# Where the two operands of every matmul lie within 128 bytes: a transformer block pair with 9,040 wide matmuls

## The chip, the cores and the metric

The kernel runs on one core of one Trainium2 chip. The metric is the device time of one execution in microseconds (us); the figure of a kernel is the median of several runs. One further execution of the kernel was profiled, and all rows below come from it. It is the same instruction stream, but its time is its own.

## The reference, cut to what matters

The reference chains two transformer blocks on 256 tokens of width 2,048, all in fp32. The first block has a projection of width 11,776, sliding-window attention, retention, a merge, and a layer ("peer") that picks 128 experts for each token out of 16,384 single-row experts. The second has a projection, an attention with forget gates, a recurrent branch, a mixture of 32 experts of width 256 in 4 groups, and a gated output.

```python
proj = xn @ w_in[layer]                                  # 256 x 2048 by 2048 x 11776
y_a = sliding_window_attention(...) @ w_attn_branch[layer]
y_r = retention(...) @ w_ret_branch[layer]
h = h + merged @ w_out[layer]
qry = (xt @ w_query).reshape(T, H, 2, PEER_HALF_DIM)     # peer: scores, top 16 of 128 twice, top 16 of 256
act = jax.nn.gelu(jnp.einsum('td,thkd->thk', xb, expert_down[ib]))
y = jnp.einsum('thk,thkd->td', gb * act, expert_up[ib])
...
for e in range(N_EXPERTS):                               # second block, 32 experts
    hid = jax.nn.silu(t @ w_gate[e]) * (t @ w_up[e])
    out = out + (hid @ w_down[e]) * comb[:, e:e + 1]
```

Nearly all of the arithmetic is these matrix products, with weights that are read from memory once.

## The kernel before, in words

**How a product is made.** Every wide product is done in three matmuls on operands that are split in two fp32r parts: a high part (`hi`) and the rest (`lo`). Activations lie in the pool `big` as split, transposed tiles (`xhi` and `xlo`, `rhi`, `mhi`, `hhi`, `zhi`, `nhi`, `yhi`, the sorted expert inputs `xs`). Weights come by DMA as fp32 tiles (`raw`, `rawg`, `rawd`) from the queue of SyncE (SP), are cast to `whi` by ScalarE (line 253) and the difference `wlo` is made by VectorE (line 254). Then TensorE runs, for each of 16 slices `k` of 128 rows and each half `t` of the tokens, lines 282 to 284:

```python
TE.matmul(ps[:, t, :], h_, hi, start=st, stop=False)
TE.matmul(ps[:, t, :], h_, lo, start=False, stop=False)
env["mm"] = TE.matmul(ps[:, t, :], l_, hi, start=False, stop=en)
```

The first operand after the output is the stationary one, 128 by 128, loaded into the array by a weight load of its own; the second is the moving one, 512 columns as a rule. So a stationary operand is a slice of an activation tile and the moving one is a slice of a weight tile. In `mm_tr` (lines 293 to 295) it is the other way round: a slice of the weights is stationary and 256 columns of activations move. The up-projection of the peer layer (`ua`, `ub`, lines 807 to 809) has dense coefficients `chi` and `clo` as stationary operands; the expert layers have `xs` (lines 1281 to 1283, output `pgu`) and the hidden layer `hhl` (lines 1306 to 1308, output `oa`). One product of the second block (`pv`, output of a 1,032-wide projection) has weight tiles of 344 columns. Attention and transposes use plain fp32 matmuls, in which one instruction of the code becomes two records.

**Stages.** In order: input projection, attention, retention, merge and output of block one (up to about 780 us of the span); the query projection `pq`; routing and the gather of single expert rows (`row`, 8 KB a token, by GpSimd's indirect DMA), with the dot products on VectorE; 32 rounds of the up-projection with gathers of 2 KB pieces (`urow`) beside it; block two's projections and attention; the 32 experts; the gated output. The program's order on each engine is fixed when it is built.

**Where tiles lie.** Pools are laid one after the other in each partition: `cst`, `big`, `sm`, `wr` (raw weights), `ws` (split weights), then what belongs to a stage: `wka`, `wkp`, `wkx`, `wkm`, `wkl` for work tiles and `wr`/`ws` of that stage. A tile of a pool starts where the one before it ends, in units of 32 bytes. Two unused pieces, `pad`, stand in `cst` (32 bytes) and `sm` (two of 32 bytes). In the built program of the kernel before, `big` starts at byte 23,040 and `wr` at byte 141,056, and every stationary and every moving operand of the fp32r matmuls starts at a multiple of 128 bytes. The one exception is `pv`: a weight tile there holds two slices of 344 columns, 1,376 bytes each, so that the second slice starts 96 bytes above a multiple of 128.

Of the kernel before, what the change touches and what calls it, by code (L numbers as in the profile page):

```python
# [9 lines left out]
F32 = mybir.dt.float32  # L10
F32R = mybir.dt.float32r
# [8 lines left out]
P = 128  # L20
# [55 lines left out]
def build(ctx: ExitStack, tc: tile.TileContext, A, out, taps=None, stop=None):  # L76
# [5 lines left out]
    cst = ctx.enter_context(tc.tile_pool(name="cst", bufs=1))  # L82
    big = ctx.enter_context(tc.tile_pool(name="big", bufs=7))
    sm = ctx.enter_context(tc.tile_pool(name="sm", bufs=2))
# [3 lines left out]
    env = {}  # L88
# [36 lines left out]


    cc = cst.tile([P, NKEEP], F32, name="cc")
    cst.tile([P, 8], F32, name="pad")
    sm.tile([P, 8], F32, tag="pad", name="pad")
    nc.sync.dma_start(cc[:, 0:128], A["c_const"][:, 0:128])  # L130
    vecs = w4([P, P], name="vecs")
    nc.scalar.dma_start(vecs[0:16, :], A["attn_norm"].rearrange("(r c) -> r c", c=P))
# [425 lines left out]
    coef = pk[:, 768:1024].rearrange("p (t k) -> p t k", t=2)  # L558
    eidx = env["wk"].tile([P, 2, 8, 16], I32, tag="eidx", name="eidx", bufs=1)
    iota16 = iota[:, 0:16]  # L560

    def route(t, hd):
        sc = sc_t[t][:, hd]
# [434 lines left out]
    for b in range(2):  # L998
# [20 lines left out]
        for hd in range(4 * b, 4 * b + 4):  # L1019
# [21 lines left out]
            PT = env["wk"].tile([P, 384], F32, tag="PT", name="PT2")  # L1041
# [145 lines left out]
    new_phase("m", raws=3, splits=1)  # L1187
    Pmm = env["wk"].tile([P, 2, 2, 512], F32R, tag="Pmm", name="Pmm", bufs=1)
    Pm = Pmm[:, 0]
    t4 = sm.tile([P, 2, 4], F32, tag="t4", name="t4")  # L1190
    V.tensor_tensor(out=t4, in0=prk[:, 0:8].rearrange("p (t g) -> p t g", t=2), in1=oh, op=ALU.mult)
    V.tensor_reduce(out=rk[:, :, 0:1], in_=t4, axis=AX.X, op=ALU.add)
# [278 lines left out]
```

## Time and profile before

| | |
|---|---|
| runs | 3,212.75, 3,214.78 and 3,214.96 us; median 3,214.78 us |
| the profiled execution | 3,219.45 us, of which the span of the program is 3,217.7 us |
| matmul records in it | 12,368 (and as many weight loads) |

How to read the rows further down: a page of the profile gives for each engine its busy time (PE is TensorE's matmuls, PEld its weight loads, DVE VectorE, ACT ScalarE, POOL GpSimd, SP SyncE), and the span in 40 equal slices with a digit for the busy tenths. PEclk is the granted clock of TensorE in tenths of its full 2.4 GHz. Windows give for one stretch its length, then busy time and number of instructions (x) of PE, PEld, DVE, ACT and POOL, then the granted clock, the mean busy share of the DMA engines and what they moved in GB/s. Waits name who waited for whom, the sum in us, how often, and the longest. Timeline rows begin with the start and the length in us. Matmuls are pipelined and their shown ends are modelled; what a matmul costs in a dense stream is the distance from its start to the next one's. Groups of instructions end with their number, the busy time and the mean in ns.

### The profile page before, as it was taken

Reading aid. Unit: us, or ns where it says so; the run is one execution under the profiler, and the core shown is the slowest. Engines: PE = TensorE matmul, PEld = TensorE weight load, DVE = VectorE, ACT = ScalarE, POOL = GpSimd, SP = SyncE. Lnnn points to the kernel's source line nnn. Section 1 sums busy time; section 2 is a strip of 40 time slices with the busy share of each in tenths; the row PEclk is TensorE's granted clock in tenths of the full one; section 3 lists DMA queues with packets and bytes.
Section 4 is the critical chain, followed back from the end, with each engine's and each line's share of the span. In section 5 each row is a group of like instructions: output and inputs, shape, how many; then the busy total and the mean of one; then the engine's idle time right before and its main releaser. Section 6 shows DMA issues by size and latency. Waiting matters only on the chain. (4 is left out here: it accounts for less than half of the span.)

```text
span 3217.7 us, 35193 instructions
## 1 busy us (share of the span) xinstructions
PE 2555.4 (79%) x12368; PEld 2141.8 (67%) x12368; DVE 2535.2 (79%) x3682; ACT 1542.9 (48%) x2212; POOL 879.8 (27%) x575
## 2 busy tenths in 40 slices
PE   8999999999910004400399999999999999999999
PEld 7788888888810003300388888889987787878777
DVE  6656544555999999999988888887575799999974
ACT  5534444444310105441244444457445677778764
POOL 0000000000376686667766666620000000000000
PEclk9999999999965555555699999999999999999999
DMA  6455555565899999999789999974654599999964
GB/s 239 151 182 162 184 191 195 187 220 197 328 352 363 331 427 387 376 342 419 285 306 334 335 334 334 334 263 142 204 190 139 201 338 348 381 344 379 348 226 167
DMA packets 302522, 898.22 MB, mean 279 GB/s; under 512 B 20736, under 2 KB 42240, under 8 KB 268288
## 3 DMA queue, kind: packets, MB, share of 16 engines
q1 hardware_dynamic: 226560, 542.88, 48.1%
q0 software_dynamic: 57760, 335.65, 27.3%
q10 hardware_dynamic: 18016, 17.35, 1.6%
q8 instruction: 99, 1.62, 0.2%
q14 instruction: 87, 0.71, 0.1%
HBM read 887.42 MB, written 8.39 MB: 278 GB/s over the span
## 5 line engine op out<-in xcount | busy, mean ns | idle before, releaser
L254 DVE TENSOR_TENSOR wlo<-raw,whi 128x1024 fp32r<-128x1024 f32 (+1 forms) x538 | 648.5, 1208 | 453.1 <-ACT whi L253 446.9
L253 ACT CAST whi<-raw 128x1024 fp32r<-128x1024 f32 (+1 forms) x538 | 559.5, 1041 | 686.9 <-PE pj L284 255.6
L621 DVE CUSTOM_DVE_ANT_0 row<-row,hn 128x2048 f32<-128x2048 f32 x256 | 579.7, 2291 | 6.1 <-DMA row<-in_peer_expert_down_dram,eidx 5.7
L612 POOL DMA_INDIRECT row<-in_peer_expert_down_dram,eidx x256 | 508.4, 1986 | 265.8 <-DVE dots L621 100.7
L199 POOL TENSOR_TENSOR r<-rstdv,mhalf 128x2 f32<-128x2 f32 x5 | 4.5, 890 | 1508.9 <-DVE rstdv L225 1508.9
L612 POOL DMA_INDIRECT urow<-in_peer_expert_up_dram,eidx x256 | 322.8, 1261 | 197.7 <-DVE h L771 143.8
L254 DVE TENSOR_TENSOR wlo<-rawg,whi 128x1024 fp32r<-128x1024 f32 x256 | 313.1, 1225 | 35.1 <-ACT whi L253 10.3
L253 ACT CAST whi<-rawg 128x1024 fp32r<-128x1024 f32 x256 | 270.0, 1056 | 97.9 <-PE pgu L1283 68.6
L282 PE MATMUL pj<-whi,xhi 128*128 128x512 f32 x736 | 289.4, 393 | 1.3 <-ACT whi L253 1.3
L283 PE MATMUL pj<-wlo,xhi 128*128 128x512 f32 x736 | 288.6, 392 | 0.0
L284 PE MATMUL pj<-whi,xlo 128*128 128x512 f32 x736 | 288.2, 392 | 0.0
L639 PE MATMUL pcf<-cc,pk 128*128 128x128 f32 x2 | 0.9, 460 | 340.7 <-DVE pk L626 340.7
L639 PEld LDWEIGHTS pcf<-cc,pk 128*128 128x128 f32 x2 | 0.4, 182 | 341.5 <-issue 177.8
L1282 PE MATMUL pgu<-wlo,xs 128*128 128x512 f32 x512 | 199.8, 390 | 3.1 <-DVE wlo L254 3.1
L1281 PE MATMUL pgu<-whi,xs 128*128 128x512 f32 x512 | 200.0, 391 | 0.0
L1283 PE MATMUL pgu<-whi,xs 128*128 128x512 f32 x512 | 199.2, 389 | 0.0
L771 DVE SCALAR_TENSOR_TENSOR h<-urow,pk,h 128x512 f32<-128x512 f32 x256 | 191.8, 749 | 4.5
L254 DVE TENSOR_TENSOR wlo<-rawd,whi 128x1024 fp32r<-128x1024 f32 x128 | 154.1, 1224 | 12.1 <-ACT whi L253 1.1
L282 PEld LDWEIGHTS pj<-whi,xhi 128*128 128x128 f32 x736 | 138.5, 188 | 29.5 <-ACT whi L253 1.7
L284 PEld LDWEIGHTS pj<-whi,xlo 128*128 128x128 f32 x736 | 138.4, 188 | 28.1
L283 PEld LDWEIGHTS pj<-wlo,xhi 128*128 128x128 f32 x736 | 138.4, 188 | 27.7
L253 ACT CAST whl<-raw 128x1024 fp32r<-128x1024 f32 x96 | 101.2, 1056 | 113.5 <-PE ua L809 83.0
(547 smaller groups left out, 6302.0 us busy)
## 6 DMA issues: line engine op xcount, KB each, us to landing
raw<-in_w_in_dram SPq DMA_DIRECT2D x124, 1024.0 KB
raw<-in_peer_expert_up_dram SPq DMA_DIRECT2D x96, 1024.0 KB
rawg<-in_w_expert_gate_dram SPq DMA_DIRECT2D x128, 512.0 KB
rawg<-in_w_expert_up_dram SPq DMA_DIRECT2D x128, 512.0 KB
rawd<-in_w_expert_down_dram SPq DMA_DIRECT2D x64, 1024.0 KB
raw<-in_w_out_dram SPq DMA_DIRECT2D x32, 1024.0 KB
raw<-in_w_ret_branch_dram SPq DMA_DIRECT2D x16, 1024.0 KB
raw<-in_w_peer_query_dram SPq DMA_DIRECT2D x16, 1024.0 KB
```

The costliest lines, as they stand in the source:

```text
L199: G.tensor_tensor(out=dst, in0=v, in1=mhalf[:, 0:n], op=ALU.pow)
L253: S.copy(hi, raw)
L254: env["last"] = V.tensor_tensor(out=lo, in0=raw, in1=hi.bitcast(F32), op=ALU.subtract)
L282: TE.matmul(ps[:, t, :], h_, hi, start=st, stop=False)
L283: TE.matmul(ps[:, t, :], h_, lo, start=False, stop=False)
L284: env["mm"] = TE.matmul(ps[:, t, :], l_, hi, start=False, stop=en)
L612: G.indirect_dma_start(out=dst, out_offset=None, in_=src, in_offset=bass.IndirectOffsetOnAxis(ap=idx, axis=0))
L621: V.tensor_tensor_reduce(out=row[:, i, :], in0=row[:, i, :], in1=hn[:, t, :], scale=1.0, scalar=0.0, op0=ALU.mult, op1=ALU.add, accum_out= ...
L771: V.scalar_tensor_tensor(out=h[:, t, 1536:2048], in0=row[:, k, :], scalar=coef[:, t, c0 + k:c0 + k + 1], in1=h[:, t, 1536:2048], op0=ALU.m ...
L1281: TE.matmul(o_, xh, hi[:, :, i, :], start=k == 0, stop=False)
L1282: TE.matmul(o_, xh, lo[:, :, i, :], start=False, stop=False)
L1283: TE.matmul(o_, xl, hi[:, :, i, :], start=False, stop=k == NK - 1)
```

## The change

The unused pieces change, and no others. In `cst` the piece grows from 32 to 96 bytes, and those of `sm` go, so that `big` starts 64 bytes later (byte 23,104) while `sm` and all behind it stay where they were. In `wkp` an unused piece of 64 bytes stands behind `eidx`, ahead of the tiles `chi` and `clo`. In `wkm` one of 64 bytes stands ahead of `esg` and `hhl`, and a second behind them, ahead of the raw and split weights of that stage; the two lines for `esg` and `hhl` in between only fix the order in which the pool lays them out.

```diff
     cc = cst.tile([P, NKEEP], F32, name="cc")
-    cst.tile([P, 8], F32, name="pad")
-    sm.tile([P, 8], F32, tag="pad", name="pad")
+
+    cst.tile([P, 24], F32, name="pad")
     nc.sync.dma_start(cc[:, 0:128], A["c_const"][:, 0:128])
...
     iota16 = iota[:, 0:16]
+    env["wk"].tile([P, 16], F32, tag="pad", name="pad", bufs=1)
...
     Pm = Pmm[:, 0]
+    for i in range(2):
+        env["wk"].tile([P, 16], F32, tag="pad%d" % i, name="pad", bufs=1)
+        if i == 0:
+            env["wk"].tile([P, 256], F32, tag="esg", name="esg")
+            env["wk"].tile([P, 2, 2, P], F32R, tag="PT", name="hhl")
```

On all five engines the instructions, their order and their waits are the same in both built programs. What differs is where operands start, counted from the last multiple of 128 bytes:

| matmuls | stationary before, after | moving before, after |
|---|---|---|
| lines 282 to 284 on `big` tiles, 512 columns | 0, 64 | 0, 0 |
| the same, `pv`, 344 columns | 0, 64 | 0 or 96, 0 or 96 |
| lines 807 to 809 (`chi`, `clo`) | 0, 64 | 0, 0 |
| lines 1281 to 1283 (`xs`), 1306 to 1308 (`hhl`) | 0, 64 | 0, 0 |
| lines 293 to 295 (`mm_tr`), 256 columns | 0, 0 | 0, 64 |
| `pxs` (256 columns), `plT` (256) | 0, 64 | 0, 0 |
| `pun` (512 columns, 64 of them) | 0, 0 | 0, 64 |
| `pu` (512 columns, 48 of them) | 0, 0 | 0, 0 |

DMAs into `big` (the gathered rows `row` and `urow` above all) start 64 bytes above a multiple of 256 after the change, and at a multiple of 256 before. The raw weights of the expert stage start 128 bytes above a multiple of 256 in three of their six buffers, and at a multiple before; the other raw tiles stay.

## Rows read from the trace of the kernel before

**Rows 1.** The page: engines' busy time, and 40 slices of the span.
```profile
PE 2555.4 (79%) x12368; PEld 2141.8 (67%) x12368; DVE 2535.2 (79%) x3682; ACT 1542.9 (48%) x2212; POOL 879.8 (27%) x575
...
PE   8999999999910004400399999999999999999999
...
PEclk9999999999965555555699999999999999999999
```

**Rows 2.** Windows by stage: PE, PEld, DVE, ACT, POOL; clock, DMA, GB/s.
```profile
80.00:780.00 700.00, 699.87 (x3159) 575.32 (x3158) 383.36 (x463) 310.34 (x373) 5.53 (x8) 1.00 0.56 184
...
880.00:1300.00 420.00, 56.64 (x281) 48.45 (x280) 415.55 (x770) 74.83 (x174) 297.96 (x148) 0.54 0.96 374
...
1590.00:2110.00 520.00, 515.99 (x2335) 428.93 (x2335) 451.66 (x682) 252.02 (x399) 330.48 (x265) 0.99 0.93 322
2110.00:2560.00 450.00, 433.96 (x2490) 380.23 (x2490) 312.21 (x565) 259.35 (x382) 12.23 (x11) 0.99 0.53 180
2560.00:3060.00 500.00, 494.92 (x2214) 404.78 (x2213) 461.02 (x444) 386.76 (x420) 0.00 (x0) 1.00 0.96 357
3060.00:3217.00 157.00, 143.06 (x621) 115.97 (x619) 100.49 (x108) 84.81 (x109) 0.69 (x1) 0.95 0.54 193
```

**Rows 3.** Waits in three stretches: first block, up-projection, experts (two rows).
```profile
ACT whi L253 <- PE pj L284: 229.5, 134, 4.6
...
ACT whi L253 <- PE ua L809: 67.8, 49, 1.7
...
ACT whi L253 <- PE pgu L1283: 79.5, 199, 4.6
...
SPq L1271 <- DVE wlo L254: 241.3, 113, 9.2
```

**Rows 4.** One window inside the input projection, 512-column matmuls alone.
```profile
545.00:613.00 68.00, 68.00 (x301) 56.31 (x300) 31.77 (x27) 28.72 (x29) 0.00 (x0) 1.00 0.58 192
```

**Rows 5.** Timeline of the up-projection: start us, length us, engine, line.
```profile
1800.18 0.39 PE L807 MATMUL ua<-whi,chi 128*128 128x512 f32 x1
1800.19 0.19 PEld L808 LDWEIGHTS ua<-wlo,chi 128*128 128x128 f32 x1
...
1800.41 0.39 PE L808 MATMUL ua<-wlo,chi 128*128 128x512 f32 x1
```

**Rows 6.** Timeline of TensorE, 256-column matmuls, eleven in a row.
```profile
2224.74 0.28 PE L294 MATMUL prg<-zlo,whi 128*128 128x256 f32 x1
...
2225.94 0.28 PE L295 MATMUL prg<-zhi,wlo 128*128 128x256 f32 x1
```

**Rows 7.** Timeline of TensorE, 512 columns just behind a break, seven matmuls.
```profile
740.61 0.39 PE L283 MATMUL pwo<-wlo,mhi 128*128 128x512 f32 x1
...
742.00 0.39 PE L283 MATMUL pwo<-wlo,mhi 128*128 128x512 f32 x1
```

**Rows 8.** Timeline of TensorE, plain fp32: two passes of 512, two of 256.
```profile
94.35 1.02 PE L426 MATMUL po<-PT,qkv_a 128*128 128x512 f32 x2
95.21 0.59 PE L410 MATMUL psc<-qkv_a 128*128 128x256 f32 x2
...
2353.96 0.59 PE L1045 MATMUL po<-PT,wv 128*128 128x256 f32 x2
2354.39 0.38 PE L1046 MATMUL po<-PT,wv 128*128 128x128 f32 x2
```

**Rows 9.** Timeline of TensorE in `pv`, 344 columns, every sixth matmul.
```profile
2262.21 0.32 PE L282 MATMUL pv<-whi,zhi 128*128 128x344 f32 x1
...
2263.15 0.32 PE L282 MATMUL pv<-whi,zhi 128*128 128x344 f32 x1
...
2264.10 0.32 PE L282 MATMUL pv<-whi,zhi 128*128 128x344 f32 x1
```

**Rows 10.** Groups of TensorE's instructions by line: number, busy us, mean ns.
```profile
L282 PE MATMUL pj<-whi,xhi 128*128 128x512 f32 x736 | 289.4, 393 | 1.3 <-ACT whi L253 1.3
...
L1281 PE MATMUL pgu<-whi,xs 128*128 128x512 f32 x512 | 200.0, 391 | 0.0
...
L295 PE MATMUL pq<-hhi,wlo 128*128 128x256 f32 x256 | 75.5, 295 | 8.6 <-DVE wlo L254 8.6
...
L293 PE MATMUL prx<-zhi,whi 128*128 128x256 f32 x128 | 37.3, 291 | 0.0
...
L282 PE MATMUL pb<-whi,aT 128*128 128x512 f32 x64 | 24.9, 389 | 0.0
```

## The prediction

> **What bounds the kernel now.** I read the page first, then windows by stage, then who waits for whom, then the timeline of TensorE alone. On the page TensorE is busy in nine tenths or more of nearly every slice up to 780 us and again from about 1,600 us; between them VectorE is, and TensorE's granted clock falls to about half, the 1.2 GHz level [rows 1]. The windows turn that into stages: TensorE covers 699.9 of 700 us in the first block, 516 of 520 in the up-projection, 434 of 450 in block two's projections, 495 of 500 in the experts and 143 of 157 at the end, all at a granted clock of 0.95 to 1.00, the 2.4 GHz level; VectorE covers 415.6 of the 420 us of the gather stage [rows 2]. The waits say the same from the other side: in the first block, the up-projection and the experts ScalarE's casts wait for TensorE to give a split buffer back, and SP waits for VectorE to free a raw buffer before it loads the next weights [rows 3]. So in about 2,300 of 3,217.7 us a faster TensorE is a faster kernel, until the next engine is reached. That is VectorE in the experts, at 461 of 500 us, and DMA there, 0.96 busy; in the first block VectorE is at 383 of 700 [rows 2].
>
> What a matmul costs there is its distance to the next. In a window of the input projection 300 weight loads, one a matmul, fit in 68.00 us: 226.7 ns each [rows 4]. The 256-column ones are 1.20 us apart over ten, 120 ns each [rows 6]. The difference, 106.7 ns for 256 columns, is 0.417 ns a column, which is the 2.4 GHz level. Both widths then have the same rest: 226.7 less 512 columns at 0.417 (213.3) is 13.3 ns, and 120 less 106.7 is 13.3 ns. This rest is the only thing that the change can touch.
>
> **What the rest may be.** Each matmul carries a weight load that starts with it and takes 0.19 us, inside the 0.23 us of its stream [rows 5]. Both read operands that lie in the same partitions. Three rows speak for a collision between them rather than a fixed cost. Just behind a break the same shape takes 1.39 us for six, 232 ns each, 5 ns more than in the steady stream [rows 7]; a fixed cost would not vary. Plain fp32 matmuls, which feed their columns at half the rate (0.86 us for two passes of 512, so 0.84 ns a column), have no such rest: passes of 256 take 0.43 us for two, half of that to the 10 ns that the rows show, with a weight load beside each as well [rows 8]. And the rest does not grow with the width, as a cost per weight load would not. One row speaks against a large effect of the address: in `pv` the moving slices of every second `k` start 96 bytes above a multiple of 128, and six matmuls take 0.94 us there and 0.95 us where they start at the multiple [rows 9], a rest of 13.3 and 15.0 ns over 344 columns (143.3 ns).
>
> The Trainium skill, in TensorE: Matmul & The Clock Gate, Step-by-step: what each phase is for, says that TensorE reads its moving and its stationary operand through two independent ports, so that loading the next weights takes nothing from the running matmul. By that rule no address matters and the sum is zero. The same page, Back-to-back issue gap, gives N/2.4 + 2.5 ns for a warm matmul alone, 216 ns for 512 columns; the trace has 226.7, so by this figure about 11 ns of the rest would be open to the change.
>
> **The change part by part.** No instruction, order or wait changes. With each edit the stationary operand goes to 64 bytes past a multiple of 128 while the moving one stays, or the reverse in `mm_tr`; the edits have one price, ns a matmul, and differ in counts.
>
> Price: no row shows operands 64 bytes apart. The bounds are nothing, which is the nearest row in address (`pv`, 96 bytes apart, hardly moved), and the whole rest of 13.3 ns, which plain fp32 shows to be possible. I take half, 6.7 ns. The rows are about equally far from both ends: a shift of 96 bytes removes 1.7 of 15 ns, and half-rate streams lose nothing.
>
> Counts: the 512-column lines come in threes, 13 groups of them, from `pj` with 736 to `pb` on `aT` with 64 [rows 10]; with all of them, the last `pgt`, `pun` and `pu` it is 9,040, less the 48 of `pu`, which the change leaves alone. 9,000 x 6.7 ns is 60 us. Nearly all of these lie in the stages that TensorE bounds.
>
> 256 columns: `prx` and `prg` have 768 of them [rows 10], 5 us. The 768 of `pq` [rows 10] run into the start of VectorE's stage, so I count half, 2.5 us. `pxs` and `plT` add 1 us, and the 288 of `pv` 2 us. Together 70 us.
>
> What of it is hidden: the experts' share is 2,300 x 6.7 = 15 us of 500. VectorE would then be at 461 of 485, 95%, and its waits are not spread evenly; DMA would go from 357 to 368 GB/s, and the gather stage shows 374 [rows 2]. In the up-projection VectorE goes from 452 to 452 of 505, 90%. I take 5 us off. Transposes, plain fp32 matmuls, scores and the gather stage gain nothing, and both operands of the attention products move together.
>
> DMA: the gathered rows now land 64 bytes past a multiple of 256. Below, nothing; above, what would make DMA the bound in the gather stage: it is 0.96 busy there [rows 2], so transfers that get dearer by up to 4% stay behind VectorE. I take nothing. ScalarE's and VectorE's reads and writes of shifted tiles: no row shows any at such an offset; I take nothing, since both idle where TensorE bounds, VectorE 39 of 500 us in the tightest such stage.
>
> Sum: 3,219.45 - 65 = 3,154 us for the profiled execution. That one lies 4.7 us above the median of the runs, 3,214.78, so the forecast for the median is **3,150 us**.
>
> **The rivals.**
> - *The rest goes nearly whole.* 11 to 13.3 ns x 9,000 is 99 to 120 us, 256 and 344 columns add 11. VectorE in the experts stops it: 26 to 30 us off 500 would leave it at 97 to 98%, so I take 10 to 15 off. About 3,108 us. For it: the plain fp32 rows. Against: `pv`.
> - *The change does not do what it says* (the address has no part in it): 3,215 us. For it: `pv`, and a rest that is the same 13.3 ns for both widths as a fixed cost would be. Against: 232 ns behind a break. It is the rule of the two ports, in TensorE: Matmul & The Clock Gate of the Trainium skill; the rest in the rows is where this case's trace doesn't yet agree.
> - *Slower: 64 bytes apart collides more than 0 apart.* The place is every 512-column stream. Each ns over 226.7 costs 9 us, and it decides from 0.7 ns on. The 232 ns behind breaks show that such spacings exist; 5 ns more give +45, with the 256-column ones +52: 3,267 us. Against: the stream settles at the lower spacing by itself.
> - *Slower by DMA.* If transfers into `big` get dearer by 12%, the gather stage is DMA's: 420 x (0.96 x 1.12 - 1) = 32 us, 3,247 us if TensorE gains nothing, and it outweighs the forecast's gain only beyond 20%. DMA: Bandwidth & Descriptors, How a descriptor splits into AXI transactions, in the Trainium skill, has transactions of 256 bytes that start at multiples of 256; an estimate from it, by a piece more for each descriptor, is 33 for 32 on the 8 KB rows and 9 for 8 on the 2 KB pieces, 3% and 12%. No row here shows a start off that grid.
>
> **How the numbers follow.** Forecast (rest cut by some 4 to 9 ns) 0.38, whole rest 0.22, no change 0.24, collides more 0.11, DMA 0.05. The forecast's own range is 3,125 to 3,185. The range of 8 in 10 takes in the whole rest on the low side, 3,100 where VectorE takes less off, and no change on the high side with the spread of the runs, 3,222; it leaves out the two slower cases (0.16) and a bit below. Measurement tells 0.2%, 6 us, from no change. Faster 0.60, same 0.24, slower 0.16.
>
> **What would show it.** In the changed profile, 300 weight loads in the input projection take 66.0 us where they took 68.00 (220 ns each); 256-column matmuls stand 113 ns apart; `pv` loses as much; the first block's window shrinks by about 20 us, the up-projection's by 15, the experts' by 12 to 15. The plain fp32 rows and the gather stage (420 us) stay. I am wrong if the spacing of 226.7 ns stays (the ports), if it drops and the experts don't shrink (VectorE or DMA took over), or if the gather stage grows.

## The result, and the profile after

| | before | after |
|---|---|---|
| median of 4 runs each, us | 3,214.87 (3,212.75 to 3,215.39) | 3,263.44 (3,261.75 to 3,263.99) |
| profiled execution, us (span) | 3,219.45 (3,217.7) | 3,262.95 (3,261.1) |

The ratio is 1.0151, with a 95% interval of 1.0134 to 1.0169: the change costs 49 us. The forecast was 3,150 us, the range ended at 3,222.

The page of the changed kernel: engines' busy time, and 40 slices of the span, as in [rows 1].
```profile
PE 2597.0 (80%) x12368; PEld 2135.0 (65%) x12368; DVE 2538.5 (78%) x3682; ACT 1539.1 (47%) x2212; POOL 878.5 (27%) x575
...
PE   9999999999920004400499999999999999999999
...
PEclk9999999999965555555699999999999999999999
```
The same 12,368 matmuls now fill 2,597 us instead of 2,555, 42 us more. VectorE's, ScalarE's and GpSimd's totals move by 4 us at most. The granted clock is at the same levels in the same slices, so the columns are not fed more slowly for the clock's sake.

Windows of the changed kernel at the places of [rows 2]: PE, PEld, DVE, ACT, POOL; clock, DMA, GB/s.
```profile
80.00:780.00 700.00, 699.98 (x3083) 561.91 (x3082) 375.50 (x455) 300.04 (x362) 5.52 (x8) 1.00 0.54 180
880.00:1300.00 420.00, 64.86 (x395) 56.80 (x393) 415.38 (x752) 77.37 (x169) 286.20 (x146) 0.57 0.97 377
1590.00:2110.00 520.00, 512.24 (x2308) 417.69 (x2309) 444.23 (x698) 244.08 (x389) 332.65 (x264) 0.99 0.89 309
...
2560.00:3060.00 500.00, 491.47 (x2196) 396.76 (x2196) 449.40 (x455) 375.84 (x418) 0.00 (x0) 1.00 0.93 342
```
In the first block TensorE is as full as before and gets through 3,083 matmuls in 700 us instead of 3,159. The experts' window has 2,196 instead of 2,214, and VectorE and DMA have more room there (449 and 0.93, before 461 and 0.96): TensorE is still what bounds. The gather stage is as it was, VectorE 415.4 of 420 us.

How far apart the matmuls stand is seen in windows inside dense streams of the changed kernel, 70 us of the input projection and 480 us of the up-projection.
```profile
560.00:630.00 70.00, 70.00 (x301) 56.40 (x301) 32.83 (x28) 28.51 (x29) 0.00 (x0) 1.00 0.56 183
1650.00:2130.00 480.00, 480.00 (x2059) 386.75 (x2058) 408.22 (x572) 220.95 (x345) 295.87 (x229) 1.00 0.93 325
```
A window also counts what already runs at its start, so 480 us go over 2,057 weight loads: 233.3 ns, where [rows 4] gave 226.7. The forecast was 220. The rest beside 512 columns (213.3 ns) has grown from 13.3 to 20 ns. Two rows of the timeline of TensorE in the changed kernel, ten 256-column matmuls apart, answer to [rows 6]:
```profile
2249.92 0.28 PE L294 MATMUL prg<-zlo,whi 128*128 128x256 f32 x1
...
2251.09 0.28 PE L295 MATMUL prg<-zhi,wlo 128*128 128x256 f32 x1
```
1.17 us over ten is 117 ns where it was 120: here the change helps. In part of `pq` it helps more; these two rows are 129 matmuls apart:
```profile
812.37 0.28 PE L293 MATMUL pq<-hhi,whi 128*128 128x256 f32 x1
...
826.99 0.28 PE L293 MATMUL pq<-hhi,whi 128*128 128x256 f32 x1
```
14.62 us over 129 is 113.3 ns; further on in `pq`, at the same places, it is 117.8. In `pv`, 344 columns, the groups of six of [rows 9] take 0.96 and 0.94 us where they took 0.94 and 0.95.
```profile
2291.72 0.32 PE L282 MATMUL pv<-whi,zhi 128*128 128x344 f32 x1
...
2292.68 0.32 PE L282 MATMUL pv<-whi,zhi 128*128 128x344 f32 x1
...
2293.62 0.32 PE L282 MATMUL pv<-whi,zhi 128*128 128x344 f32 x1
```
Over all 288 of these matmuls the slices of even `k` go from 158.3 to 160.0 ns each and those of odd `k` from 157.2 to 156.7: they move, one way and the other, and the product as a whole keeps its spacing (157.7 and 158.3 ns).

Where the time came from, by the starts of first and last matmuls in the two timelines (us):

| stretch | before | after | difference |
|---|---|---|---|
| first `pj` to first `pq` (block one) | 770.9 | 790.3 | +19.4 |
| first to last `pq` | 115.9 | 111.1 | -4.8 |
| last `pq` to first `ua` (routing, gather) | 713.0 | 716.9 | +3.9 |
| first `ua` to last `ub` (up-projection) | 526.8 | 540.3 | +13.5 |
| last `ub` to first `pgu` (block two) | 395.5 | 396.0 | +0.5 |
| first `pgu` to last `oa` (experts) | 569.0 | 579.4 | +10.4 |
| last `oa` to last `pgt` | 108.4 | 109.6 | +1.2 |

The sum is +44, and the spans differ by 43.4. The medians differ by 49, since the profiled execution of before lay 4.6 us above its median and that of after 0.5 below. One row of the table is not what it seems: the 115.9 us of `pq` before are the longest of the twelve kernels profiled (the two sweeps further down left aside). The others, also those where 256 columns stand 120 ns apart as before, have 110.4 to 113.4 us, so the -4.8 can't be put down to the spacing.

### The profile page after: what moved, and what is told of

It is laid out like the page before. It is cut to its first block, busy times and chain, and to the rows that moved or that the text cites. A ratio compares the mean times of both kernels' runs of the same rounds, so it can differ in the third digit from the quotient of the medians.

```text
span 3261.1 us, 35193 instructions
## 1 busy us (share of the span) xinstructions
PE 2597.0 (80%) x12368; PEld 2135.0 (65%) x12368; DVE 2538.5 (78%) x3682; ACT 1539.1 (47%) x2212; POOL 878.5 (27%) x575
## 5 line engine op out<-in xcount | busy, mean ns | idle before, releaser
L613 POOL DMA_INDIRECT row<-in_peer_expert_down_dram,eidx x256 | 498.0, 1945 | 275.5 <-DVE dots L622 103.1
L613 POOL DMA_INDIRECT urow<-in_peer_expert_up_dram,eidx x256 | 332.0, 1297 | 200.3 <-DVE h L772 148.5
```

The source lines that it names most:

```text
L613: G.indirect_dma_start(out=dst, out_offset=None, in_=src, in_offset=bass.IndirectOffsetOnAxis(ap=idx, axis=0))
```

## The experiments

My theory after the result (A): what counts is the offset of the two operands of a matmul from one another, and 64 bytes is worse than 0 for 512 columns. Its rivals: only the stationary operand's own place counts (B); any operand off a multiple of 128 costs (C); a cause outside the matmuls, such as DMA into `big`. "Offset" below is the stationary operand's start less the moving one's. A spacing is the time from the first to the last start in a stretch without a break, over the number of intervals.

### Which operand, and one part alone

The moving operands at 64 and `big` at 0 (`e1_moving64`), against the kernel before:
```diff
-    sm.tile([P, 8], F32, tag="pad", name="pad")
+    sm.tile([P, 16], F32, tag="pad", name="pad")
```


> Here it is the split weights that start 64 bytes past a multiple of 128 and the tiles in big that stay at a multiple, the other way round than in the change; the operands chi, clo and hhl move along with the weights, so that in the up-projection (2,304 matmuls) and in the down half of the experts (768) both start at 64. Theory A, the offset of one operand from the other decides: about 233 ns between 512-column matmuls wherever they are 64 apart (5,856 of them, +39 us), 226.7 ns in the up-projection and in the experts' down half, 256 columns somewhat faster as in the change (-10): 3,240 to 3,255 us. Theory B, only the stationary operand's own place counts: 226.7 ns for the 5,856, 233 ns in the up-projection and the down half (+20 us): about 3,235 us, slow where A is fast. Theory C, any operand off a multiple of 128 costs: 233 ns everywhere, 3,275 us.

Both at 64 (`e2_both64`):
```diff
-    cst.tile([P, 8], F32, name="pad")
+    cst.tile([P, 24], F32, name="pad")
```


> Both operands of every matmul start 64 bytes past a multiple of 128, and the gathered rows land 64 past a multiple of 256 as in the change. Theory A (the offset between the two decides): the steady spacing is 226.7 ns again and 256 columns stand 120 ns apart, 3,215 us. Theory B (the stationary operand's own place): 233 ns for all 9,000, and no gain at 256 columns, about 3,275 us. Theory C (any operand off the multiple): 3,275 us or more. If the landing place of the DMAs has a price beside, the gather stage grows over 420 us here too.

The change's first edit alone (`e5_big64`), and `big` at 32 (`e3_big32`):
```diff
-    cst.tile([P, 8], F32, name="pad")
-    sm.tile([P, 8], F32, tag="pad", name="pad")
+    cst.tile([P, 24], F32, name="pad")                             # e5_big64
+    cst.tile([P, 16], F32, name="pad")                             # e3_big32
+    sm.tile([P, 8], F32, tag="pad", name="pad", bufs=1)            # e3_big32
```


> One part of the change alone: the edit of the pools cst and sm, so that big starts at 64; chi, clo and hhl stay at multiples of 128. If the price is per matmul and per place, 5,856 of the 512-column matmuls go to 233 ns (+39 us), the 256-column ones gain some 10 us as in the change, and the up-projection and the experts' down half stay at 226.7 ns: 3,240 to 3,250 us, 15 to 20 us less than the whole change. A cause that lies outside these matmuls (DMA into big) would leave the whole 49 us: 3,263 us.

> Stationary operands in big start 32 bytes past a multiple of 128, moving ones of 512 columns at a multiple, the up-projection and the experts' down half untouched at 0 and 0. If the price falls off evenly between 0 and 64 bytes apart: about 230 ns for the 5,856 (+20 us), 3,225 to 3,235 us. If what counts is which 64-byte half of 128 bytes the two operands lie in, 32 is as 0: 226.7 ns, 3,215 us. If any offset but 0 costs the same: 233 ns, 3,245 us.

| kernel | median, us | ratio to before (95%) | input projection, ns | up-projection, ns |
|---|---|---|---|---|
| moving at 64 | 3,223.95 | 1.0034 (1.002 to 1.0049) | 228.9 | 226.7 (both at 64) |
| both at 64 | 3,219.37 | 1.002 (1.001 to 1.003) | 226.7 | 226.7 |
| `big` alone at 64 | 3,251.27 | 1.0116 (1.01 to 1.0133) | 233.3 | 226.7 (both at 0) |
| `big` alone at 32 | 3,247.42 | 1.0103 (1.0086 to 1.012) | 233.3 | 226.7 (both at 0) |

The windows of the input projection and of the up-projection, columns as above: first with the moving operands at 64,
```profile
546.00:616.00 70.00, 70.00 (x308) 57.43 (x307) 32.66 (x28) 29.02 (x31) 0.00 (x0) 1.00 0.57 192
1650.00:2130.00 480.00, 480.00 (x2119) 397.48 (x2118) 415.51 (x583) 226.22 (x349) 293.71 (x235) 1.00 0.96 336
```
then with both at 64,
```profile
545.00:615.00 70.00, 70.00 (x311) 57.96 (x310) 33.00 (x27) 29.30 (x30) 0.00 (x0) 1.00 0.56 194
1650.00:2130.00 480.00, 480.00 (x2119) 397.52 (x2118) 415.15 (x581) 225.51 (x346) 292.93 (x234) 1.00 0.96 335
```
and with `big` alone at 64.
```profile
556.00:626.00 70.00, 70.00 (x302) 56.40 (x301) 31.97 (x27) 28.60 (x29) 0.00 (x0) 1.00 0.55 188
1650.00:2130.00 480.00, 480.00 (x2120) 397.44 (x2119) 417.56 (x590) 228.66 (x358) 296.61 (x236) 1.00 0.96 334
```
In the same 70 us stand some 310, 307 and 301 matmuls. Both at 64 have the spacing of both at 0, in the kernel with everything moved (226.7 ns) and within the first of these kernels, whose up-projection has both at 64 and holds 2,119 matmuls in 480 us. That excludes B and C. `big` alone leaves the up-projection at its old spacing and costs 38 us, 11 less than the whole change, near the 13.5 us of the up-projection above; and with both at 64 the DMAs land as in the change, and all but 6 us of the 49 are gone. So the bulk has no cause outside the matmuls (the 6 us are taken up further down). A stands, but not as I had put it: I had taken offsets of +64 and -64 for the same, and they are not (233.3 and 228.9 ns), so that its 3,240 to 3,255 us for the moving operands at 64 missed the 3,224 measured. And 32 bytes cost as much as 64; the expectations of a price that falls off evenly, and of one that goes by 64-byte halves, both failed.

### A map of offsets

The sweep moves the split weights of each product in turn (the time of this kernel means nothing, since the experts have a pair of split buffers less):
```diff
+            o, w = (0, 1024) if env["ph"] == "x" else (8 * env["sw"], 1088)
...
-            hi = ws.tile(shape, F32R, tag="hi", name=nm + "hi")
+            hi = ws.tile([P, w], F32R, tag="hi", name=nm + "hi")[:, o:o + n]
...
     def mm_nat(ps, xhi, xlo, W, c0, c1, k0=0, nk=NK, xk=lambda k: k, first=True, last=True, loaded=()):
+        env["sw"] = (env.get("sw", -1) + 1) % 8
```


> A sweep, read by its spacing and not by its time (the experts have one pair of split buffers less here, so that they starve). Every product in turn gets its split weights 0, 32, 64, ... 224 bytes past a multiple of 256, while the tiles in big stay at a multiple of 256; one product of the input projection is 96 matmuls at one offset. If only the difference of the two places modulo 128 counts: 226.7 ns at 0 and 128, 229.0 at 64 and 192 (moved weights, as in the run that moved them by 64), 233.3 at 96 and 224 (which is the stationary operand 32 bytes ahead). If modulo 256 counts: 229.0 at 64, 233.3 at 192 and 224 (the stationary operand 64 and 32 bytes ahead, as in the change and in the run with big at 32), and 32, 96, 128 and 160 are new; one of them may lie below 226.7 ns. If the sign of the offset counts because the two operands are read in a fixed order, the spacing rises on one side of 0 alone. Of the 256-column products in pq the same: 120 ns at 0, 114 to 118 ns at 64.

The timeline of TensorE in this kernel, first and last matmul of two products of 96, at offset 192 and at offset 64:
```profile
444.91 0.40 PE L292 MATMUL pb<-whi,rhi 128*128 128x512 f32 x1
...
466.66 0.40 PE L294 MATMUL pb<-whi,rlo 128*128 128x512 f32 x1
...
523.88 0.39 PE L292 MATMUL pb<-whi,rhi 128*128 128x512 f32 x1
...
546.05 0.39 PE L294 MATMUL pb<-whi,rlo 128*128 128x512 f32 x1
```
21.75 us over 95 intervals is 229 ns, 22.17 is 233.4. All eight places, read like that:

| offset modulo 256, bytes | 0 | 32 | 64 | 96 | 128 | 160 | 192 | 224 |
|---|---|---|---|---|---|---|---|---|
| 512 columns, ns (sweep) | 226.8 | 233.3 | 233.3 | 234.3 | 233.2 | 233.4 | 229.0 | 233.4 |
| 512 columns, ns (kernels above) | 226.7 | 233.3 | 233.3 | | | | 228.9 | |
| 256 columns in `pq`, ns | 119.7 | | 114.9 | 118.5 | 118.6 | 119.9 | 117.3 | 117.0 |

(The 256-column values at 0, 64 and 224 are of the kernels before, with moving at 64 and with `big` at 32.) The map goes by 256 bytes: 128 is as bad as the others, and 192 is what the moving operand 64 ahead gave. In the kernel before, the offsets of the 512-column matmuls are 0, 256, 512 and 768 modulo 1,024, and [rows 4] shows one spacing for all, so beyond 256 bytes nothing counts. For 512 columns 0 is the best place of the eight; for 256 columns it is among the worst.

The map also explains a number above that I had not foreseen. In the changed kernel the experts' own split weights start 128 bytes further, by the second unused piece of `wkm`, so the matmuls on these weights have offset 64 - 128, that is 192. The stage's own pair of split buffers is one of three that are used in turn, so that is a third of the experts' matmuls. By the trace that third of `pgu` takes 229.5 ns and the others 232.5, and the experts lose 10.4 us, not the 15 of 2,300 matmuls at 233.3.

A test of the map on a layout that it had not seen, without any unused piece (`n1_nopads`):
```diff
-    cst.tile([P, 8], F32, name="pad")
-    sm.tile([P, 8], F32, tag="pad", name="pad")
```


> The kernel before without its two unused pieces: big starts 96 bytes past a multiple of 128 and the weights 32, so stationary operands stand 64 bytes ahead of the moving ones (modulo 256) for the 5,856 products on big, with neither at a multiple of 128; the up-projection and the experts' down half have both at 32, offset 0. If only the offset counts, at steps of 32 bytes: 233.3 ns for the 5,856 and 226.7 ns in the up-projection, and 3,251 us, the time with big alone at 64 (ratio 1.010 to 1.013). If the own place counts beside it: another spacing in the up-projection, where both operands lie at 32.

3,253.36 us, ratio 1.0119 (1.0102 to 1.0137). Its windows:
```profile
556.00:626.00 70.00, 70.00 (x302) 56.40 (x301) 32.10 (x27) 28.51 (x29) 0.00 (x0) 1.00 0.56 186
...
1650.00:2130.00 480.00, 480.00 (x2119) 397.61 (x2118) 418.60 (x591) 228.67 (x358) 298.77 (x237) 1.00 0.96 334
```
As forecast: 301 in 70 us where the operands are 64 apart, 2,119 in 480 us where both lie at 32.

A finer sweep (`s2_fine`), with the list of starts in place of the steps of 32 bytes and the coefficient tiles moved in the up-projection:
```diff
+SWL = (1, 2, 4, 6, 10, 12, 14, 18, 20, 28, 0, 52, 58, 60, 62, 63)
...
+        so = SWL[ig % 16]
+        hi, lo = (w4([P, 4 * T + 64], F32R, n)[:, so:so + 4 * T].rearrange("p (i t) -> p i t", i=4)
+                  for n in ("chi", "clo"))
```


> A finer sweep, read by its spacing and not by its time (the experts starve as in the first sweep). The split weights of one product in turn start 4, 8, 16, 24, 40, 48, 56, 72, 80, 112, 0, 208, 232, 240, 248 and 252 bytes past a multiple of 256, in the up-projection the coefficient tiles instead by the same amounts. From the first sweep: 226.7 ns at 0, 229.0 where the moving operand is 64 ahead, 233 to 234 at the six other multiples of 32. If the reads go by units of 32 or 64 bytes and the offset within a unit is nothing: 4 to 24 bytes as 0, 226.7 ns, and 72 to 80 as 64. If the two reads collide by time, with a period of 256 bytes: a steady rise from 226.7 at 0 to 233 at 32, and perhaps a spacing below 226.7 between two of the first sweep's points. If only an exact 0 is good: 233 ns from 4 bytes on.

With the stationary operand moved: 232.3 ns at 4 bytes, 230.7 at 8, 233.4 at 16, 230.0 at 24, 228.3 at 240, 233.3 at 248 and 226.7 at 252. With the moving operand moved: 237.5 ns at 4, 232.8 at 8, 231.6 at 16, and 227.8 at 252. The timeline of TensorE, 95 matmuls apart with the moving operand at 0, and 79 apart with it at 4 bytes:
```profile
605.10 0.39 PE L293 MATMUL pb<-whi,rhi 128*128 128x512 f32 x1
...
626.63 0.39 PE L295 MATMUL pb<-whi,rlo 128*128 128x512 f32 x1
...
733.39 0.39 PE L294 MATMUL pwo<-wlo,mhi 128*128 128x512 f32 x1
...
752.16 0.40 PE L295 MATMUL pwo<-whi,mlo 128*128 128x512 f32 x1
```
21.53 us over 95 is 226.6 ns, 18.77 over 79 is 237.6. None of the three expectations fits: the spacing neither rises steadily nor goes by units, and below 32 bytes the offset alone is not enough (stationary 4 below a multiple of 256: 226.7; moving 4 above: 237.5, the same offset). No place beats 226.7 ns.

### What in the pair collides

The up-projection in eight parts (`x1_up`): clo alone moved, and stationary slices of 64 and of 32 columns.
```diff
+UPV = ((0, 0, 128), (0, 16, 128), (0, 0, 64), (16, 16, 64),
+       (0, 0, 32), (16, 16, 32), (16, 16, 128), (0, 0, 128))
...
-                    h_, l_ = chl[0][:, k, t * P:(t + 1) * P], chl[1][:, k, t * P:(t + 1) * P]
+                    o_ = o_[0:mw]
+                    h_, l_ = chl[0][:, k, t * P:t * P + mw], chl[1][:, k, t * P:t * P + mw]
```


> The up-projection alone is changed, in eight parts of four rounds (288 matmuls each): as before; only clo 64 bytes ahead; stationary slices of 64 columns instead of 128 at offset 0, then at 64; of 32 columns at 0, then at 64; 128 columns at 64; as before. Slices of 64 and 32 columns leave out the results for the other tokens of each half, so only the spacing is read. Theory A1, the weight load for the next matmul reads beside the running stream and the two collide by their offset: with 64 and 32 columns the load reads half and a quarter as much, so the rest at offset 0 (13.3 ns) and the 20 ns at 64 shrink, to some 220 ns or less at 32 columns; and with only clo shifted the matmul that runs before clo's (line 808) is followed late, 233 ns, the other two 226.7. Theory A2, a matmul's own pair counts (the stream against its own stationary operand): with only clo shifted it is clo's matmul (line 809) that takes 233 ns. Theory D, the rest is a fixed handover that the offset only quantises: 226.7 and 233 ns whatever the number of columns of the stationary slice.

Windows of this kernel: as before; clo alone; 64 columns at 0 and at 64; 32 columns at 0.
```profile
1625.00:1670.00 45.00, 45.00 (x201) 37.24 (x200) 39.09 (x57) 21.64 (x35) 28.20 (x22) 1.00 0.95 332
1690.00:1735.00 45.00, 45.00 (x197) 36.56 (x196) 37.83 (x55) 21.05 (x34) 27.94 (x22) 1.00 0.95 323
1755.00:1800.00 45.00, 45.00 (x197) 26.28 (x196) 38.52 (x56) 21.69 (x35) 29.00 (x23) 1.00 0.95 333
1825.00:1870.00 45.00, 45.00 (x195) 26.13 (x194) 37.69 (x54) 21.38 (x35) 26.80 (x22) 1.00 0.94 329
1890.00:1935.00 45.00, 45.00 (x196) 21.19 (x195) 37.77 (x55) 21.07 (x34) 27.83 (x22) 1.00 0.93 323
```
A weight load takes 186 ns of 128 columns, 134 of 64 and 109 of 32 (PEld's time over its number). So much less is read, and yet the spacing at offset 0 does not fall: 226.7, 229.9 and 231.6 ns. At offset 64 it is 233.3, 232.6 and 231.7, so that with 32 columns the offset no longer counts. The picture that I carried from the prediction, the whole rest as time lost to two streams of reads that collide, would have less rest where less is read; it falls (A1's first half), and D's fixed handover, which no number of columns should touch, falls too. What is left of the picture is the part that hangs on the offset: 64 costs 6.6 ns over 0 with 128 columns, 2.7 with 64 and 0.1 with 32. These runs don't exclude a collision as its cause, and don't show one: a narrower slice changes more than the amount that is read. With clo alone moved the spacings behind lines 807, 808 and 809 are 228.3, 229.2 and 235.8 ns: the matmul that uses clo pays most, as A2 says and not A1, but the other two pay too, which neither has. Why an offset costs what it costs stays open.

### What 256 columns could give, and the landing place of DMAs

Four more kernels. The control `b0_pool` opens the two base pairs of split buffers with each stage and makes them 256 bytes longer in one, `b1_pq64` uses that room to move `pq`'s weights by 64 bytes:
```diff
-    ws0 = ctx.enter_context(tc.tile_pool(name="ws", bufs=2))
...
+        ws0 = phase.enter_context(tc.tile_pool(name="ws" + name + "0", bufs=2, reuse_waits="tile"))
...
+            o, w = (16 if env["off"] else 0, 1088 if env["ph"] == "p" else 1024)     # b0_pool: 0
```


> The control of the next run: the two base pairs of split buffers are opened anew with each stage instead of once, and in the stage of pq and of the up-projection they are 256 bytes longer each, so that a part of them can be used off its start; no operand of an fp32r matmul moves off a multiple of 256 from its partner. Spacings as before (226.7 and 120 ns). 3,214 us if opening the buffers anew costs nothing, some us more if it adds waits where two stages meet.

> As the control, but the split weights of pq, stationary there, start 64 bytes past a multiple of 128, and nothing else does: the offset that the run with moved weights showed to be better for 256 columns. Spacing in pq 115 ns instead of 120 (5 ns x 768 = 4 us off the stretch of pq); all 512-column ones at 226.7. If the stretch of pq sets when VectorE's stage starts: 4 us less than the control, 3,210 us. If routing and gathering start with pq's first part and run at their own pace: no difference.

Both operands at 64 once more, and both at 128 (`cst.tile([P, 40], ...)`):

> The run with both operands at 64 again, with more rounds: it was 0.2% above before (interval 0.1 to 0.3%) although its spacings are those of before. If the landing place of the gathered rows, 64 bytes past a multiple of 256, has a price of its own: 1.002 again. If that was the spread of the runs: 1.000.

> All operands and landing places 128 bytes further than before (cst's unused piece is 160 bytes), nothing relative to one another. By the offset alone: spacings and time as before, 1.000. If landing off a multiple of 256 costs the DMAs something, whatever the distance: 1.002 here as well. If only a landing off a multiple of 128 does: 1.000 here and 1.002 with both at 64.

| kernel | median, us | ratio to before (95%) |
|---|---|---|
| control | 3,219.5 | 1.0017 (1.0009 to 1.0026) |
| `pq` 64 apart | 3,219.85 | 1.0017 (1.0008 to 1.0025) |
| both at 64 | 3,220.64 | 1.002 (1.0011 to 1.0029) |
| both at 128 | 3,220.37 | 1.0016 (1.0007 to 1.0025) |

The timeline of TensorE inside `pq`: two rows of the control, 181 matmuls apart,
```profile
794.97 0.29 PE L302 MATMUL pq<-hhi,wlo 128*128 128x256 f32 x1
...
816.69 0.28 PE L300 MATMUL pq<-hhi,whi 128*128 128x256 f32 x1
```
and two of the kernel with `pq` 64 apart, 176 apart.
```profile
797.61 0.28 PE L301 MATMUL pq<-hlo,whi 128*128 128x256 f32 x1
...
817.56 0.28 PE L300 MATMUL pq<-hhi,whi 128*128 128x256 f32 x1
```
21.72 us over 181 is 120 ns, 19.95 over 176 is 113.4. The spacing falls, and the time does not. `pq` itself takes 111.3 us in the control and 111.9 here, since TensorE waits there for VectorE's `wlo` (9.3 and 9.9 us), and from the first `pq` to the first `ua` it is 825.4 and 825.7 us. `prx` and `prg` (768 matmuls at some 2 ns) would give 1.7 us, below what a measurement tells; so I have no version that beats the kernel before.

All four stand 5.5 to 6.6 us above it. For the control and the kernel built on it the trace shows a delay of their own. Two rows of TensorE before, and two of the control, where block one ends and `pq` begins:
```profile
781.32 0.39 PE L284 MATMUL pwo<-whi,mlo 128*128 128x512 f32 x1
781.55 0.28 PE L293 MATMUL pq<-hhi,whi 128*128 128x256 f32 x1
```
```profile
780.77 0.39 PE L291 MATMUL pwo<-whi,mlo 128*128 128x512 f32 x1
...
789.12 0.58 PE L300 MATMUL pq<-hhi,whi 128*128 128x256 f32 x1 [1.67 <-ACT whi L260]
```
Block one is done at the same time, and `pq` begins 7.6 us later: with the buffers opened anew, 24 transposes (`ptr`, `psk`) that stood among the first matmuls of `pq` come ahead of it and wait for VectorE. That fits the "some us more" of the control's expectation. So the control says nothing on the landing place.

With both operands moved together `pq` begins as before (781.7 and 781.9 us), and another stretch is longer. From the last `pq` to the first `ua`, routing and gather, it is 713.0 to 714.1 us in the five profiled kernels whose gathered rows land at a multiple of 256 bytes, and 715.9 to 717.6 in the seven where they don't (32, 64, 128 or 224 bytes past one). From the first `pq` on it is 824.4 to 828.9 and 827.8 to 830.0; the 828.9 are those of before, with its long `pq`. VectorE's waits for these rows from 800 to 1,640 us, before, with both at 64 and with both at 128:
```profile
DVE row L621 <- DMA row<-in_peer_expert_down_dram,eidx: 5.7, 14, 1.3
```
```profile
DVE row L621 <- DMA row<-in_peer_expert_down_dram,eidx: 8.4, 14, 2.2
```
```profile
DVE row L621 <- DMA row<-in_peer_expert_down_dram,eidx: 7.5, 16, 1.5
```
Over all twelve kernels that is 5.7 to 6.7 us against 7.1 to 8.4. So the expectation by which a landing off a multiple of 256 costs something at any distance fits (1.002 and 1.0016): the profiles, one of each kernel, show some 3 us of it, and where the other 3 of the 6 us lie stays open. The changed kernel's rows land 64 bytes off too, and its routing and gather are 3.9 us longer; block one, the up-projection, the experts and the end make 44.5 us of its 49.

## Why the prediction was wrong

- **What bounds the kernel**: right. TensorE bounds the stages named, a change of spacing came out as time in the first block, the up-projection and the experts, and ScalarE's casts still wait for TensorE (for `pj` 242.1 us in the window of the first block, 229.5 before [rows 3]). The window of the experts shows VectorE with more room, not less.
- **What a matmul costs, and what the rest is**: the arithmetic of 226.7 = 213.3 + 13.3 was right, and so was that the rest depends on where the operands lie. Right for the wrong reason: I read it as a collision at offset 0 that an offset could only lessen. By the map, offset 0 is the best place for 512 columns, and by the run with short slices the rest at offset 0 doesn't shrink when less is read.
- **The price, the step that failed**: "The bounds are nothing ... and the whole rest of 13.3 ns, which plain fp32 shows to be possible. I take half, 6.7 ns." The price is 6.6 ns of the other sign. The lower bound was no bound: the rest is what remains at one place, and no row of 512 columns showed another place, so a loss had to be in it. The nearest row for a loss stood in the text, 232 ns just behind a break [rows 7]; I used it as evidence that the rest can shrink, and only in a rival as evidence that it can grow. None of the prediction's signs of being wrong was a spacing that grows.
- **`pv` as the nearest row in address**: its second slices stand at offset 160, and with 512 columns that place costs 6.7 ns. With 344 columns it gains 1.1 (157.2 ns against 158.3 over the whole product; the 1.7 ns of the prediction were one step of the timeline's 0.01 us over six matmuls). Width decides as much as place does, so a row of 344 columns was no neighbour of one of 512.
- **The counts** held, with the other sign: block one +19.4 us for a forecast of -20, the up-projection +13.5 for -15, the experts +10.4 for -12 to -15 (a third of their matmuls is at offset 192).
- **256 columns**: gain forecast 6.7 ns a matmul, measured 2 to 6.6. The half of `pq`'s gain that I counted came to nothing: with `pq` alone moved its spacing fell, and neither its stretch nor the kernel got shorter.
- **DMA, ScalarE, VectorE at nothing**: nearly. The gather stage kept its 415 us of VectorE in 420, but with rows that land off a multiple of 256 bytes routing and gather as a whole are some 3 us longer, and VectorE waits longer for the rows.
- **The rivals**: what happened is the third, "64 bytes apart collides more than 0 apart", which I gave 0.11 and 3,267 us: its price of 5 ns was 6.6 in the run, and its loss at 256 columns was a gain. The rule of the two ports (the Trainium skill, TensorE: Matmul & The Clock Gate, Step-by-step: what each phase is for), from which I took that no address matters and that the time stays at 3,215 us, didn't carry that: in these runs the address alone moves the spacing from 226.7 to 233.3 ns. The rival by DMA was right in its sign at most: 3 us, not 32. Whether that comes from the rule that it named (the Trainium skill, DMA: Bandwidth & Descriptors, How a descriptor splits into AXI transactions) no run here shows.

## What to carry to other kernels

A rest that the profile shows at one place says nothing on which side the other places lie: when a change moves a dense stream to a place that no row has, both signs belong in the bounds, and the chance of a loss is not that of a side case. Where a kernel runs many wide fp32r matmuls, look at the start of stationary and moving operands modulo 256 bytes in the built program, and measure one stream with the offset moved before moving pools: here 7 ns on 227 was most of the 1.5% that the kernel lost, from pieces of a few dozen bytes. And an unused piece in a pool may be what holds an alignment: without the two small ones the kernel before takes 38 us more.

## What the runs showed of the hardware that was not expected

- The spacing of 512-column fp32r matmuls depends, at steps of 32 bytes, on the operands' offset modulo 256 bytes, with one good place (0: 226.7 ns), one middling (192: 229.0) and 233 to 234 at the other multiples of 32. The sign of the offset counts.
- The same offset works the other way round on another width: 64 apart, either way, brings 256 columns from 120 to between 113 and 118 ns. 344 columns move both ways: 158.3 ns at offset 0, 160.0 at 64, 157.2 at 160 and 156.7 at 224.
- A shorter weight load (109 instead of 186 ns) doesn't bring the matmuls closer: 231.6 instead of 226.7 ns at offset 0 (32 columns instead of 128).
- A moving operand that starts 4 bytes past a multiple of 256 gives 237.5 ns, the largest spacing seen.
- Gathered rows that land off a multiple of 256 bytes make routing and gather 715.9 to 717.6 us long where it is 713.0 to 714.1 (one profile of each kernel).
